# Expert rows of one group by gather from DRAM instead of by matmul, and the last pair's output in three column ranges

## The chip, the cores and the metric

The kernel runs on one core of a Trainium2 chip. The metric is the device time of one execution in microseconds (us), the median of several; lower is better. The engines are TensorE (PE; its weight loads, PEld, run beside the matmuls), VectorE (DVE), ScalarE (ACT), GpSimd (POOL) and SyncE (SP), which here only issues DMAs. Sixteen DMA engines move data between DRAM and the on-chip memory SBUF.

## The reference

One decoder block on 512 tokens of width 1024, float32. Only its last part is touched by the change: a hierarchical mixture of experts over normalised rows, top-1 of 4 groups and then top-2 of 8 SwiGLU experts in it, 32 experts in all, and the final RMSNorm.

```python
x = x + hier_moe(rmsnorm(x, g_moe[l]), ...)
return rmsnorm(x, g_final)

def run_block(args):            # in hier_moe: e expert, tok its tokens, w their weights
    e, tok, w = args
    xb = xt[tok]
    hid = jax.nn.silu(xb @ w_gate[e]) * (xb @ w_up[e])
    return (hid @ w_down[e]) * w[:, None].astype(xb.dtype)
```

Each expert has 1024 x 512 gate and up matrices and a 512 x 1024 down matrix: 6 MB in float32, 201 MB for all 32.

## The kernel before, in words

The order of all instructions on every engine is that of the program text. SBUF blocks of 4 KB a partition (`blk`) come from one pool of 48 (`NB`), middling tiles (`med`) from a pool of 13 (`MB`); an instruction that writes a new tile waits until the earlier user of its buffer is done.

After attention and memory attention the four token tiles `x_sb[t]` (128 tokens x 1024) stay in SBUF, with their scale `r2[t]` (the reciprocal root mean square), and `xrh`, `xrl`, the scaled rows split into a high and a low part. Each expert has 64 slots (`CAP`). `code` holds for each token the code of its two slots, `cw[0]` the same codes broadcast over the partitions, `sid` the code that belongs to each slot.

Experts are worked in 16 pairs (`NP`). Two pairs form a group of 4 experts, 256 slots. For each pair `p`:

- **gate and up**: 8 steps `k`, each with 8 matmul instructions for the pair's two experts (`gate_up`, tile `gu_ps`).
- **hidden**: Silu on ACT, a product on DVE (`hidden`), four transposes (`hidden_t`, tile `ht_ps`). Meanwhile PE does the previous pair's `combine`: products of the slot matrix `ot` with the output rows, split in high and low (`c_ps`), which DVE adds to `x_sb`.
- **down**: 32 instructions (`down`, tile `y_ps`).

The rows of a group (`xT`, features on the partitions) are made by `gather`: for each of 8 feature blocks, 8 matmul instructions of 256 columns take `xrh` and `xrl` times the one-hot matrix `oh` (tile `g_ps`), and ACT scales the result with the gain. Four of the eight blocks are done in the hidden part of the odd pair before the group, four among the first `k` steps of the even pair. Group 0's rows are made before the first pair.

SP issues the expert weights in blocks of 512 KB (tile `we`), 24 for a pair in the order in which they are used: 16 of gate and up, in which each two `k` steps take four blocks, then 8 of down. `eload` lets them run 33 to 35 blocks ahead (`DEPTH`). Experts with more than 64 tokens are finished in a loop (`overflow`, lines 1266 to 1296) that stands at pair 15, `k` = 2 (`SPILL`), and runs zero times in the profiled execution; the third number of `SPILL`, 372, is the count of weight blocks issued before it. The last 12 blocks are issued behind it.

In the last pair the output is made in two halves of 512 columns: down, split, products, addition to `x_sb`, the squares for the final norm, then the scale `r`, and each half of each token tile is written out by a DMA of 256 KB, the low half from ACT's queue, the high half from SP's.

Of the kernel before, what the change touches and what calls it, by code (L numbers as in the profile page):

```python
# [10 lines left out]
F32 = mybir.dt.float32  # L11
# [10 lines left out]
P = 128  # L22
# [21 lines left out]
def _shape_constants():  # L44
    p = np.arange(P)
    tri = ((p[:, None] <= p[None, :]) & (p[:, None] // 64 == p[None, :] // 64)).astype(np.float32)
    upper = (p[:, None] < p[None, :]).astype(np.float32)
    jcode = np.array([ESTR * e + s for e in range(4) for s in range(CAP)], np.int16).view(np.float32)
    e512 = np.arange(NE, dtype=np.float32) * ESTR
    row = np.concatenate([jcode, e512, np.arange(NE, dtype=np.float32), np.arange(NX, dtype=np.float32)])  # L50
    keep = np.concatenate(
        [np.eye(P, dtype=np.float32), np.tile(row, (P, 1)), (ESTR * (p // CAP) + p % CAP).astype(np.float32)[:, None]], axis=1
    )
    onehot = np.zeros((P, 256), np.float32)
    bucket = _t5_buckets()
    for u in range(256):
        onehot[bucket[255 - u], u] += 1.0
        onehot[31, u] -= 1.0
    early = np.concatenate([tri, upper, onehot], axis=1)
    return np.ascontiguousarray(keep), np.ascontiguousarray(early)  # L60


# [8 lines left out]
def block_kernel(ctx, tc, x, mem, g_mem, rel_bias, g_mix, w_in, w_alpha_up, b_alpha, g_gla_head, w_proj_gla,  # L71
# [19 lines left out]
    def blk(name, shape, dt=F32):  # L91
        return bp.tile([P] + list(shape), dt, tag="b", name=name)
# [45 lines left out]
    def tcol(t):  # L138
        return slice(t * P, (t + 1) * P)
# [110 lines left out]
    pslot = keep[:, 320 + NX:321 + NX]  # L250
    first, route = cut(blk("first", [D])), cut(blk("route", [D]))
    early = first([512])
    SY.dma_start(early, c_early)
    tri = early[:, 0:128]
    wup = first([256])[0:17, :]
    SY.dma_start(wup[0:16, :], w_alpha_up)
# [684 lines left out]
    def load_down(e, to=None):  # L941
        for q in range(4):
            b = to[q % len(to)].rearrange("p k n -> p (k n)") if to else blk("we", [D])
            SY.dma_start(b.rearrange("p (k n) -> p k n", k=1), wexp(w_exp_down, e, q, q + 1))
            yield b


    blocks = [[] for _ in range(NE)]
    eloads, elimit = [0], [SPILL[2]]

    def load_pairs():
        for p in range(NE // 2):
            pair = 2 * p, 2 * p + 1
            for loads, n in ((load_gate_up, 2), (load_down, 1)):
                each = [loads(e) for e in pair]
                for q in range(4):
                    for e, load in zip(pair, each):
                        for b in islice(load, n):
                            blocks[e].append(b)
                            yield  # L960
# [184 lines left out]
    S.activation(small("warm", [1]), neghalf[:, 0:1], AF.Silu)  # L1145


    spilled = []

    def spill_list():  # L1150
# [43 lines left out]
    def gather(oh, xT, ns, to=None):  # L1194

        for k in range(KD):
            if len(xT) == k:
                xT.extend(rows2("xT", 4, ns))
            o = to[k % 2] if to else ps("g_ps", [ns])
            for t in range(NT):  # L1200
                for q, src in enumerate((xrh, xrl)):
                    mm(o, src[t][:, tcol(k)], oh[:, t, :], t == 0 and q == 0, t == NT - 1 and q == 1)
            S.activation(xT[k], o, AF.Copy, scale=gfeat[:, k:k + 1])  # L1203
            yield

    def slot_rows(codes, n=P, oa=None):
# [34 lines left out]
    def down(y_ps, hid_t, ft, ws, cs=(0, 1)):  # L1241
        for c in cs:
            for i, (w, own) in enumerate(zip(ws, halves)):
                mm(y_ps[c][own], hid_t[:, ft, 64 * i:64 * i + 64], w[8 + ft][:, 512 * c:512 * c + 512], ft == 0,
                   ft == 3, skip_group_check=True)

    def rows_hilo(y, n=P, parts=None):
        parts = [a[0:n] for a in parts or (med("yh", [512], F32R), med("yl", [512], F32R))]
        split(*parts, y[0:n])
        return parts  # L1250

    def product(o, ot, t, y, first=True):
        for i in range(2):
            mm(o, ot[:, tcol(t)], y[i], first and i == 0, i == 1)
# [42 lines left out]

    NP = NE // 2
    slot, spill = None, spill_list()
    comb, gat = iter(()), iter(())  # L1300
    for p in range(NP):
        w = blocks[2 * p:2 * p + 2]
        used = 24 * p
        depth = DEPTH[min(p, 1)]
        if p == SPILL[0] - 1:
            n_extra = nc.values_load(spilled[0][0:1, 0:1], min_val=0, max_val=NX - 1, skip_runtime_bounds_check_because=
                                     "2 T assignments fill fewer than NX whole blocks")
        eload(used + depth)
        gu = [ps("gu_ps", [512]) for q in range(2)]
        s0 = (p % 2) * P  # L1310
        for k in range(KD):
            if (p, k) == SPILL[0:2]:
                overflow(n_extra, *spilled)
                elimit[0] = 12 * NE
            if p % 2 == 0:
                steps(gat, 1)
            gate_up(gu, k, [xT[k][:, s0 + CAP * i:s0 + CAP * i + CAP] for i in range(2)], w)
            if k % 2:
                eload(used + depth + 2 * (k + 1))
            if p == 0 and k >= BC_AT:  # L1320
                next(bcast, None)
                if k == BC_AT + 1:
                    slot = slot_rows(sid[:, 0:1])
            if p % 2 and p + 1 < NP and k == OH_AT:
                oh_next = group_hots((p + 1) // 2)
        if p % 2 and p + 1 < NP:
            xT = []
            gat = gather(oh_next, xT, 4 * CAP)
        if p == NP - 1:
            gf = blk("gf", [D])  # L1330
            SY.dma_start(gf, bcast_rows(g_final, D))
        hid = hidden(gu, slot[1])
        gs = 1 if p % 2 and p + 1 < NP else 0
        steps(gat, gs)
        steps(comb, 2 if gs else 4)
        hid_t = hidden_t(hid)
        for i in range(3):
            steps(gat, gs)
            steps(comb, 2)
        drain(comb)  # L1340
        ot = slot[0]
        if p + 1 < NP:
            slot = slot_rows(sid[:, 2 * p + 2:2 * p + 3])
        if p >= 2:
            next(spill, None)
        y_ps = [ps("y_ps", [512]) for c in range(2)]
        if p == NP - 1:
            break
        for ft in range(4):
            down(y_ps, hid_t, ft, w)  # L1350
            eload(used + depth + 16 + 2 * (ft + 1))
        ys = {c: rows_hilo(y_ps[c]) for c in range(2)}
        comb = combine(ot, ys)


    ssq, xg, r = [small("ss2", [2]) for t in range(NT)], {}, {}

    def x_half(t, c):
        return x_sb[t][:, 512 * c:512 * c + 512]

    def last_products(c):

        y = rows_hilo(y_ps[c])
        yield
        o = [ps("c_ps", [512]) for t in range(NT)]
        for t in range(NT):
            product(o[t], ot, t, y)
        yield
        for t in range(NT):
            xs = x_half(t, c)  # L1370
            V.tensor_tensor(xs, o[t], xs, op=ALU.add)
            if c == 0 and t == NT - 1:
                yield
            S.activation(blk("sqj", [512]), xs, AF.Square, scale=1.0 / math.sqrt(D), accum_out=ssq[t][:, c:c + 1])
            if c == 0:
                xg[t] = blk("xg", [512])
                G.tensor_tensor(xg[t], xs, gf[:, 0:512], op=ALU.mult)

    def scale(t):
        ms = small("ms", [1])  # L1380
        V.scalar_tensor_tensor(ms, ssq[t][:, 0:1], EPS, ssq[t][:, 1:2], op0=ALU.add, op1=ALU.add)
        r = small("rr", [1])
        G.tensor_tensor(r, ms, neghalf[:, 0:1], op=ALU.pow)
        return r

    def finish(t, r):
        o = blk("xo", [512])
        V.scalar_tensor_tensor(o, x_half(t, 1), r, gf[:, 512:1024], op0=ALU.mult, op1=ALU.mult)
        SY.dma_start(out[tcol(t), 512:1024], o)
        S.activation(xg[t], xg[t], AF.Copy, scale=r)  # L1390
        S.dma_start(out[tcol(t), 0:512], xg[t])

    part = [last_products(c) for c in range(2)]
    for ft in range(4):
        down(y_ps, hid_t, ft, w, (0,))
    next(part[0])
    for ft in range(2):
        down(y_ps, hid_t, ft, w, (1,))
    next(part[0])
    for ft in range(2, 4):  # L1400
        down(y_ps, hid_t, ft, w, (1,))
    next(part[0])
    next(part[1])
    drain(part[0])
    drain(part[1])
    for t in range(NT + 1):
        if t < NT:
            r[t] = scale(t)
        if t:
            finish(t - 1, r[t - 1])  # L1410


WIDE = 2, 2, 2, 2
SPILL = 15, 2, 372
MEM_AT, WOS = (0, 1), {5: 4, 6: 4}
LATE = [], [], range(4)
BC_AT = 2
# [38 lines left out]
```

## Time and profile before

| | |
|---|---|
| time, median of 3 | 970.77 us (969.45 to 970.99) |
| profiled execution, its own time | 969.94 us |
| its span, first to last instruction | 968.1 us |
| granted TensorE clock, mean | 0.997 |
| PE busy | 949.3 us (98%) |
| DVE, ACT, POOL busy | 471.4, 312.2, 32.6 us |
| DMA | 252.47 MB, 261 GB/s over the span |

The expert stage goes from about 486 to 968 us. A busy PE says that some matmul was under way, not that it ran at its peak. The share of DMA in a stretch is the packets' time as a share of 16 engines' time; it can come out a little above 1.

### The profile page before, as it was taken

The page shows a single profiled execution, that of the slowest core. Times are in us where ns is not written, and L with a number is a line of the kernel's source. Part 1 is how long each engine was busy: PE and PEld are TensorE (multiplying, and loading weights), DVE is VectorE, ACT ScalarE, POOL GpSimd, SP SyncE. Part 2 cuts the span into 40 slices and gives each one's busy share as a digit, 9 for nine tenths or more (in the row PEclk, how much of TensorE's full clock was granted, in tenths as well). Part 3 has the DMA queues.
Part 4 walks back from the last instruction along what each step waited for, and adds up shares of the span by engine and source line. Part 5 has one row for each costly group of instructions (what it writes and reads, how often), then busy time and mean ns, then how long its engine had stood idle before and what let it go on. Part 6 is the DMA issues. An engine that isn't in the chain of part 4 may idle for free.

```text
span 968.1 us, 13248 instructions
## 1 busy us (share of the span) xinstructions
PE 949.3 (98%) x4969; PEld 619.2 (64%) x4969; DVE 471.4 (49%) x1047; ACT 312.2 (32%) x639; POOL 32.6 (3%) x46
## 2 busy tenths in 40 slices
PE   9999999999999999999999999999999999999995
PEld 7888888878878888888835445454454543545432
DVE  5344872554557846466733254341544414344234
ACT  6452643545565424455321102111021110201103
POOL 3200010000000000000000000000000000000003
PEclk9999999999999999999999999999999999999998
DMA  9512347223253605482689999999999999999983
GB/s 296 171 44 64 68 68 194 65 66 88 66 196 131 196 1 153 124 336 92 260 339 409 408 409 409 409 409 410 408 410 409 409 408 408 409 408 409 409 317 147
DMA packets 114086, 252.47 MB, mean 261 GB/s; under 512 B 10310, under 2 KB 55651, under 8 KB 114020
## 3 DMA queue, kind: packets, MB, share of 16 engines
q1 hardware_dynamic: 113444, 250.55, 70.2%
q10 hardware_dynamic: 576, 1.05, 0.3%
q8 instruction: 40, 0.66, 0.3%
q14 instruction: 26, 0.21, 0.1%
HBM read 247.90 MB, written 3.67 MB: 260 GB/s over the span
## 4 chain that ended last, share of the span: by engine, by line
PE 92%; DVE 3%; ACT 3%; DMA 1%; issue 1%; ACTq 0%; SPq 0%; DVEq 0%
PE gu_ps L136 22%; PE y_ps L136 12%; PE fo L131 8%; PE fo L133 7%; PE fo L132 7%; PE g_ps L136 7%; PE c_ps L136 6%; PE ro L133 3%; PE ro L131 3%; PE ro L132 3%; PE x2o L136 2%; PE xo L132 1%; PE xo L133 1%; PE xo L131 1%; PE mo_ps L136 1%; PE s_ps L136 1%
## 5 line engine op out<-in xcount | busy, mean ns | idle before, releaser
L136 PE MATMUL gu_ps<-we,xT 128*64 128x512 f32 x1024 | 229.0, 595 | 0.4 <-ACT xT L1045 0.3
L136 PEld LDWEIGHTS gu_ps<-we,xT 128*64 128x64 f32 x1024 | 71.0, 137 | 134.0 <-issue 121.5
L206 DVE TENSOR_TENSOR wlo<-wraw,whi 128x1024 fp32r<-128x1024 f32 (+1 forms) x71 | 86.2, 1231 | 77.2 <-ACT whi L205 76.9
L136 PE MATMUL y_ps<-we,hid_t 128*64 128x512 f32 x512 | 114.2, 596 | 0.7 <-ACT hid_t L1238 0.7
L1230 DVE SCALAR_TENSOR_TENSOR hid<-hid,ws,gu_ps 128x512 f32<-128x512 f32 x16 | 12.0, 747 | 171.2 <-PE gu_ps L136 171.2
L131 PE MATMUL fo<-hTh,whi 128*128 128x512 f32 x224 | 89.1, 398 | 0.0
L132 PE MATMUL fo<-hTl,whi 128*128 128x512 f32 x224 | 87.5, 390 | 0.0
L133 PE MATMUL fo<-hTh,wlo 128*128 128x512 f32 x224 | 87.4, 390 | 0.0
L1263 DVE TENSOR_TENSOR x<-c_ps,x 128x512 f32<-128x512 f32 x120 | 75.0, 683 | 20.7 <-PE c_ps L136 20.7
L136 PEld LDWEIGHTS y_ps<-we,hid_t 128*64 128x64 f32 x512 | 35.9, 137 | 69.8 <-issue 60.0
L205 ACT ACTIVATE whi<-wraw 128x1024 fp32r<-128x1024 f32 (+2 forms) x73 | 74.8, 1045 | 4.2 <-DMA wraw<-in_w_in_dram 4.1
L136 PE MATMUL g_ps<-oh,xrh 128*128 128x256 f32 x256 | 66.0, 299 | 1.4 <-DVE oh L1028 1.4
L136 PEld LDWEIGHTS g_ps<-oh,xrh 128*128 128x128 f32 x256 | 47.0, 189 | 30.7 <-issue 24.3
L136 PE MATMUL g_ps<-oh,xrl 128*128 128x256 f32 x256 | 61.6, 281 | 0.0
L1229 ACT ACTIVATE hid<-gu_ps 128x512 f32<-128x512 f32 x16 | 9.6, 597 | 156.8 <-PE gu_ps L136 156.8
L205 ACT ACTIVATE yh<-y_ps 128x512 fp32r<-128x512 f32 x32 | 19.1, 598 | 115.1 <-PE y_ps L136 115.1
L1203 ACT ACTIVATE xT<-g_ps,gfeat 128x256 f32<-128x256 f32 x56 | 25.8, 474 | 89.2 <-PE g_ps L136 57.6
L136 PE MATMUL c_ps<-yh,ot 128*128 128x512 f32 x128 | 52.0, 406 | 0.7 <-ACT yh L205 0.7
L136 PE MATMUL c_ps<-yl,ot 128*128 128x512 f32 x128 | 50.6, 395 | 0.2 <-DVE yl L206 0.2
L131 PEld LDWEIGHTS fo<-hTh,whi 128*128 128x128 f32 x224 | 42.1, 188 | 10.1 <-issue 1.9
L133 PEld LDWEIGHTS fo<-hTh,wlo 128*128 128x128 f32 x224 | 42.0, 188 | 9.1
L136 PEld LDWEIGHTS g_ps<-oh,xrl 128*128 128x128 f32 x256 | 47.1, 189 | 0.6
(321 smaller groups left out, 1487.4 us busy)
## 6 DMA issues: line engine op xcount, KB each, us to landing
we<-in_w_exp_gate_dram SPq DMA_DIRECT2D x128, 512.0 KB, 10.2
we<-in_w_exp_up_dram SPq DMA_DIRECT2D x128, 512.0 KB, 10.2
we<-in_w_exp_down_dram SPq DMA_DIRECT2D x128, 512.0 KB, 10.2
wraw<-in_w_in_dram SPq DMA_DIRECT2D x38, 512.0 KB, 4.1
wraw<-in_w_out_dram SPq DMA_DIRECT2D x8, 512.0 KB, 5.5
wraw<-in_w_ckv_dram SPq DMA_DIRECT2D x8, 512.0 KB, 4.8
wraw<-in_w_proj_gla_dram SPq DMA_DIRECT2D x4, 512.0 KB, 4.3
wraw<-in_w_proj_moba_dram SPq DMA_DIRECT2D x4, 512.0 KB, 4.4
```

The source lines that it names most:

```text
L131: PE.matmul(o, lh, rh, start=first, stop=False)
L132: PE.matmul(o, lh, rl, start=False, stop=False)
L133: PE.matmul(o, ll, rh, start=False, stop=last)
L136: PE.matmul(o, l, r, start=first, stop=last, **kw)
L205: S.activation(hi, src, AF.Copy)
L206: eng.tensor_tensor(lo, src, f(hi), op=ALU.subtract)
L1203: S.activation(xT[k], o, AF.Copy, scale=gfeat[:, k:k + 1])
L1229: S.activation(row, gu[0][0:n], AF.Silu)
L1230: V.scalar_tensor_tensor(row, row, ws[:, 0:1], gu[1][0:n], op0=ALU.mult, op1=ALU.mult)
L1263: V.tensor_tensor(xs, o, xs, op=ALU.add)
```

## The change

For group 1 (`FETCH`), the scaled rows are written to a DRAM tile `xd` and fetched by token number. ACT makes the rows (`write_rows`) at `k` = 1 to 4 of pair 0, and POOL issues the four writes of 512 KB. A table of token numbers (`tokens`, 256 KB) is loaded by POOL. `fetch` finds on DVE the token of each slot and lets POOL issue one indirect DMA of 128 rows for pair 2 (at pair 0, `k` = 7) and one for pair 3 (at pair 1, `k` = 7), 512 KB each. `turn` transposes the rows on PE in the hidden part of the pair before, two to a step, and ACT scales them with the gain. `gather` and its one-hots are left out for this group. The other groups are as before.

The 372 becomes 376, so four more blocks, the last of gate and up, are issued ahead of the loop. The last pair's down weights come as 8 blocks of two row blocks and 512 columns, first all of the low columns. Its output is worked in column ranges of 512, 256 and 256, the additions and squares are reordered, and three token tiles are written in one DMA of 512 KB each, the fourth in halves.

```diff
+    def load_down_halves(e):
+        for c in range(2):
+            for q in range(2):
+                b = blk("we", [2, 512])
+                rows = w_exp_down[0][e][2 * q * P:(2 * q + 2) * P, 512 * c:512 * c + 512]
+                SY.dma_start(b, rows.rearrange("(k p) n -> p k n", p=P))
+                yield b
...
-            for loads, n in ((load_gate_up, 2), (load_down, 1)):
+            for loads, n in ((load_gate_up, 2), (load_down_halves if p == NE // 2 - 1 else load_down, 1)):
...
+    xd = dp.tile([T, D], F32, name="xd")
+    tok = med("tok", [T])
+    G.dma_start(tok, c_early[:, 512:])
+
+    def write_rows(t):
+        xp = blk("xp", [D])
+        S.activation(xp.rearrange("a (q j p) -> a q j p", p=P, j=2), paired(x_sb[t]), AF.Copy, scale=r2[t])
+        G.dma_start(xd[tcol(t), :], xp)
...
+    def fetch(codes):
+        oa, ws, idx = med("oa", [T]), small("ws", [2]), small("idx", [1], I32)
+        for i in range(2):
+            V.scalar_tensor_tensor(oa, cw[0][:, i, :], codes, tok, op0=ALU.is_equal, op1=ALU.mult,
+                                   accum_out=ws[:, i:i + 1])
+        V.tensor_tensor(idx, ws[:, 0:1], ws[:, 1:2], op=ALU.add)
+        b = blk("rows", [D])
+        G.indirect_dma_start(b, None, xd[:, :], bass.IndirectOffsetOnAxis(ap=idx[:, 0:1], axis=0))
+        return b
+
+    def turn(rows, xT):
+        b = blk("xT", [KD, P])
+        xT.extend(b[:, k, :] for k in range(KD))
+        for k in range(0, KD, 2):
+            t_ps = ps("xt_ps", [2, P])
+            for j in range(2):
+                PE.transpose(t_ps[:, j, :], rows[:, tcol(k + j)], ident)
+            for j in range(2):
+                S.activation(xT[k + j], t_ps[:, j, :], AF.Copy, scale=gfeat[:, k + j:k + j + 1])
+            yield
...
+            if p == 0 and 1 <= k <= NT:
+                write_rows(k - 1)
+            if (p + 2) // 2 in FETCH and k == 7:
+                fetched[p + 2] = fetch(sid[:, 2 * p + 4:2 * p + 5])
-            if p % 2 and p + 1 < NP and k == OH_AT:
+            if p % 2 and p + 1 < NP and k == OH_AT and (p + 1) // 2 not in FETCH:
                 oh_next = group_hots((p + 1) // 2)
-        if p % 2 and p + 1 < NP:
+        if (p + 1) // 2 in FETCH:
+            xT = []
+            gat = turn(fetched.pop(p + 1), xT)
+        elif p % 2 and p + 1 < NP:
...
+    ranges = (0, 512), (512, 256), (768, 256)
...
+    last_down(0, range(4))
+    high(0)
+    low(0)
+    last_down(1, range(4))
+    high(1)
+    low(1)
+    last_down(2, range(2))
+    o0 = products(0)
+    o1 = products(1)
+    last_down(2, range(2, 4))
+    for t in range(NT):
+        add(o0, 0, t)
+        square(0, t)
+        gains(t)
+    for t in range(NT):
+        add(o1, 1, t)
+        if t == 1:
+            high(2)
+        square(1, t)
+        if t == 2:
+            low(2)
+    o2 = products(2)
+    for t in range(NT):
+        add(o2, 2, t)
+        square(2, t)
+        if t >= 2:
+            scale(t - 2)
+    for t in range(NT):
+        if t == 0:
+            scale(2)
+        low_half(t)
+        high_half(t)
+        if t == 0:
+            scale(3)
+        if t + 1 < NT:
+            SY.dma_start(out[tcol(t), :], xo[t])
+    S.dma_start(out[tcol(t), 0:512], xo[t][:, 0:512])
+    SY.dma_start(out[tcol(t), 512:], xo[t][:, 512:])
...
-SPILL = 15, 2, 372
+FETCH = (1,)
+SPILL = 15, 2, 376
```

## Rows read from the trace of the kernel before

**Rows 1.** Table by stretch, the expert stage; last: PE clock, DMA share, GB/s.
```profile
482.00:488.00 6.00, 4.71 (x32) 3.47 (x34) 4.50 (x19) 3.38 (x9) 0.00 (x0) 1.00 0.33 104
488.00:500.00 12.00, 12.00 (x60) 4.23 (x58) 3.21 (x8) 2.04 (x4) 0.00 (x0) 1.00 1.00 382
500.00:915.00 415.00, 413.38 (x2073) 192.67 (x2070) 162.99 (x336) 59.89 (x113) 0.00 (x0) 1.00 1.03 409
```

**Rows 2.** Waits of SP's queue, 565 to 915: us in total, times, longest.
```profile
SPq L938 <- DMA we<-in_w_exp_down_dram: 83.4, 94, 1.6
```

**Rows 3.** Timeline of SP: weight blocks 48, 360, 371, 372, the last eight.
```profile
502.41 0.38 SPq L938 DMA_DIRECT2D we<-in_w_exp_gate_dram  x1
...
903.32 0.33 SPq L938 DMA_DIRECT2D we<-in_w_exp_gate_dram  x1
...
918.12 0.33 SPq L938 DMA_DIRECT2D we<-in_w_exp_up_dram  x1
928.32 0.33 SPq L938 DMA_DIRECT2D we<-in_w_exp_gate_dram  x1
...
930.40 7.32 SPq L944 DMA_DIRECT2D we<-in_w_exp_down_dram  x8
```

**Rows 4.** DMA issues on the page: KB each, us from issue to landing.
```profile
we<-in_w_exp_up_dram SPq DMA_DIRECT2D x128, 512.0 KB, 10.2
```

**Rows 5.** Chain that ended last, pairs 1 to 3: start us, us.
```profile
511.08 13.73 PE gu_ps L136 x64
524.81 1.15 PE g_ps L136 x8
...
526.88 0.44 PE ht_ps L1236 x4
527.32 0.96 PE g_ps L136 x8
...
539.97 1.15 PE g_ps L136 x8
...
570.35 13.73 PE gu_ps L136 x64
```

**Rows 6.** The same chain, pair 15.
```profile
925.32 3.46 PE gu_ps L136 x16
...
929.93 7.41 DMA we<-in_w_exp_up_dram
...
937.38 2.79 PE gu_ps L136 x10
940.17 2.05 PE c_ps L136 x8
...
944.50 5.87 PE y_ps L136 x24
```

**Rows 7.** Waits of SP's queue, 915 to 940, at the loop.
```profile
SPq L1267 <- PEq L1267: 7.5, 2, 7.3
```

**Rows 8.** Timeline of ACT at the start of pair 0.
```profile
485.77 1.57 ACT L1045 ACTIVATE xT<-g_ps,gfeat 128x256 f32<-128x256 f32 x4
```

**Rows 9.** Instructions of line 925: ns least, median, most.
```profile
L925 ACT ACTIVATE xrh<-x,rr x4: 1217/1220/1222, 443.9 to 476.2; 128x1024 fp32r<-128x1024 f32 x4
```

**Rows 10.** Timeline of POOL from 480; in brackets its idle time before.
```profile
951.90 5.01 POOL L1377 TENSOR_TENSOR xg<-x,gf 128x512 f32<-128x512 f32 x4 [475.74 <-DVE x L1371]
```

**Rows 11.** Timeline of the last part.
```profile
953.05 0.61 ACT L1374 ACTIVATE sqj<-x 128x512 f32<-128x512 f32 x1
...
960.23 3.11 SPq L1389 DMA_DIRECT2D out_dram<-xo  x4
...
963.69 0.34 ACTq L1391 DMA_DIRECT2D out_dram<-xg  x1
```

**Rows 12.** Table by stretch, the output written from two queues.
```profile
962.00:963.00 1.00, 0.00 (x0) 0.00 (x0) 0.79 (x2) 0.58 (x2) 0.00 (x0) 0.81 1.04 385
966.00:967.00 1.00, 0.00 (x0) 0.00 (x0) 0.00 (x0) 0.00 (x0) 0.00 (x0) 0.50 0.62 225
```

More of the change, by code (lines that the diff above doesn't have):

```diff
@@ L58, in _shape_constants @@
         onehot[31, u] -= 1.0
-    early = np.concatenate([tri, upper, onehot], axis=1)
+    tokens = np.tile(np.arange(T, dtype=np.float32), (P, 1))
+    early = np.concatenate([tri, upper, onehot, tokens], axis=1)
     return np.ascontiguousarray(keep), np.ascontiguousarray(early)
@@ L252, in block_kernel @@
     early = first([512])
-    SY.dma_start(early, c_early)
+    SY.dma_start(early, c_early[:, 0:512])
     tri = early[:, 0:128]
@@ L1299, in block_kernel @@
     slot, spill = None, spill_list()
-    comb, gat = iter(()), iter(())
+    comb, gat, fetched = iter(()), iter(()), {}
     for p in range(NP):
@@ L1309, in block_kernel @@
         gu = [ps("gu_ps", [512]) for q in range(2)]
-        s0 = (p % 2) * P
+        s0 = 0 if p // 2 in FETCH else (p % 2) * P
         for k in range(KD):
@@ L1332, in block_kernel @@
         hid = hidden(gu, slot[1])
-        gs = 1 if p % 2 and p + 1 < NP else 0
+        gs = 1 if (p % 2 or p // 2 in FETCH) and p + 1 < NP else 0
         steps(gat, gs)
@@ L1353, in block_kernel @@
         comb = combine(ot, ys)
[L1356 to L1365, printed above, removed]
-        for t in range(NT):
[L1367 to L1377, printed above, removed]
+    ranges = (0, 512), (512, 256), (768, 256)
@@ new lines, in block_kernel, with x_part, y_part, last_down @@
+    ssq, xo = [small("ss4", [4]) for t in range(NT)], [blk("xo", [D]) for t in range(NT)]
+    r = [small("rr", [1]) for t in range(NT)]
+    for t in range(NT):
+        V.memset(ssq[t][:, 3:4], EPS)
+    y_ps.append(ps("y_ps", [256]))
+    def x_part(i, t):
+        a, n = ranges[i]
+        return x_sb[t][:, a:a + n]
+    def y_part(i):
+        return y_ps[i][:, 0:ranges[i][1]]
+    def last_down(i, fts):
+        a, n = ranges[i]
+        c, a = divmod(a, 512)
+        for ft in fts:
+            for e, (b, own) in enumerate(zip(w, halves)):
+                mm(y_ps[i][own, 0:n], hid_t[:, ft, 64 * e:64 * e + 64], b[8 + 2 * c + ft // 2][:, ft % 2, a:a + n],
+                   ft == 0, ft == 3, skip_group_check=True)
@@ new lines, in block_kernel, with high, low, products @@
+    y = [[med(q, [n], F32R) for q in ("yh", "yl")] for _, n in ranges]
+    def high(i):
+        S.activation(y[i][0], y_part(i), AF.Copy)
+    def low(i):
+        V.tensor_tensor(y[i][1], y_part(i), f(y[i][0]), op=ALU.subtract)
+    def products(i):
+        n = ranges[i][1]
+        o = [ps("c_ps", [512 // n, n]) for _ in range(NT * n // 512)]
+        o = [b[:, q, :] for b in o for q in range(512 // n)]
+        for t in range(NT):
+            product(o[t], ot, t, y[i])
+        return o
@@ L1379, in scale, with add, square, gains @@
+    def add(o, i, t):
+        V.tensor_tensor(x_part(i, t), o[t], x_part(i, t), op=ALU.add)
+    def square(i, t):
+        S.activation(blk("sqj", [512])[:, 0:ranges[i][1]], x_part(i, t), AF.Square, scale=1.0 / math.sqrt(D),
+                     accum_out=ssq[t][:, i:i + 1])
+    def gains(t):
+        G.tensor_tensor(xo[t][:, 0:512], x_part(0, t), gf[:, 0:512], op=ALU.mult)
     def scale(t):
         ms = small("ms", [1])
-        V.scalar_tensor_tensor(ms, ssq[t][:, 0:1], EPS, ssq[t][:, 1:2], op0=ALU.add, op1=ALU.add)
@@ L1382, in scale @@
[L1382 to L1410, printed above, removed]
+        V.tensor_reduce(ms, ssq[t], axis=AX.X, op=ALU.add)
+        G.tensor_tensor(r[t], ms, neghalf[:, 0:1], op=ALU.pow)
@@ new lines, in low_half, with high_half @@
+    def low_half(t):
+        S.activation(xo[t][:, 0:512], xo[t][:, 0:512], AF.Copy, scale=r[t])
+    def high_half(t):
+        V.scalar_tensor_tensor(xo[t][:, 512:], x_sb[t][:, 512:], r[t], gf[:, 512:], op0=ALU.mult, op1=ALU.mult)
+    last_down(0, range(4))
[12 more added lines that the diff above has]
+        gains(t)
@@ new lines, in block_kernel @@
+    for t in range(NT):
[11 more added lines that the diff above has]
+            scale(t - 2)
+    for t in range(NT):
+        if t == 0:
[6 more added lines that the diff above has]
+            SY.dma_start(out[tcol(t), :], xo[t])
```

## Prediction

> **What bounds the kernel now.** I read the page first, then the table by stretch, the chain that ended last, the waits of SP's queue and its timeline. The page alone misleads: PE is busy for 98% of the span, so it looks like the one bound, and taking matmuls from it looks like a gain of their full length. The table by stretch says that the DMA engines are full as well: from 500 to 915 us their share is 1.03 at 409 GB/s, while from 488 to 500 they moved 382 GB/s and from 482 to 488 only 104 [rows 1]. At 409 GB/s a weight block of 524,288 bytes takes 1.28 us. SP's waits say the same from the other side: between 565 and 915 its queue stood for earlier weight blocks, 83.4 us of it for one kind of them alone, hardly for PE [rows 2].
>
> So two streams run side by side, and what counts is which is ahead. PE takes a pair of experts in half of 570.35 − 511.08, that is 29.6 us [rows 5]; DMA needs 24 blocks × 1.28 = 30.8. PE is the faster one and lives on blocks that were loaded ahead. Block 48, the first of pair 2, is issued at 502.41 [rows 3] and lands 10.2 later [rows 4], at 512.6; PE uses it from 541.1, behind the gather piece at 539.97 [rows 5]: 28.5 us in hand. Block 360, the first of pair 15, is issued at 903.32 [rows 3], lands at 913.5 and is used at 925.32 [rows 6]: 11.8 us in hand. 13 pairs ate 16.7 us of the lead.
>
> In pair 15 the lead ends. Block 371 is issued at 918.12 and 372 only at 928.32 [rows 3], since the last 12 stand behind the loop, where SP waits 7.3 us for PE [rows 7]. Block 375, the last of gate and up, lands at 929.93 + 7.41 = 937.3, and PE's last 10 gate-and-up instructions hang on it: they start at 937.38, and the pair's first combine product follows at 940.17, the down part at 944.50 [rows 6]. From there to the end of the span (968.1) it is 23.6 us.
>
> **The gather of group 1.** Removed: eight pieces of 8 matmuls, four in the hidden part of pair 1 (1.15, then three at 0.96) and four at 1.15 in pair 2 [rows 5], together 8.6 us. Added: 16 transposes, at 0.44 for four [rows 5] 1.8 us, and some 0.6 for eight changes between kinds of matmul: 2.4 (bounds 1.8 and 3.0). PE is then 6.2 us earlier from pair 3 on (5.6 to 6.8). That is a gain only as far as weights are there.
>
> **The DMAs that come with it.** Four writes of 512 KB, two gathers of 512 KB: 3.15 MB. The 256 KB of token numbers come before pair 0, where the engines are little used (482 to 488, [rows 1]); nothing waits for them before the first fetch, so I cost them at nothing, and at 0.6 us without that cover. The writes can't come there: ACT makes the rows in program order behind the xT scaling that begins at 485.77 [rows 8], the first about 489, and each takes about the 1.22 of the like instruction [rows 9]. They meet full engines. No row shows POOL issuing a DMA. The nearest is the output, where two queues write together: share 1.04, 385 GB/s [rows 12], not more than the 409 of one. So I take the queues as sharing one capacity: 3.15 MB / 409 = 7.7 us, less 0.4 for the room between 382 and 409 in 488 to 500 (12 us × 27 GB/s is 0.3 MB, 0.8 us; I take half), so 7.3 us by which every later weight block is late. Bounds: 0, if a second queue could add its bytes to the first one's; 10, if the writes run at 385 (8.2) and four buffers lent to the rows leave the engines without a load for 2 us. I take the sharing, because the row with two queues is the nearest there is.
>
> Here a rule speaks against the change. The Trainium skill, DMA: Bandwidth & Descriptors, section "Issuing engines are not separate DMA queues", says that transfers started by SP, ACT or POOL run on the same 16 engines and interleave, so another issuer saves issue time alone. The output row agrees (385 with two queues). By that rule the added bytes cost 7.7 us of the stream; with queues of their own capacity they would cost nothing.
>
> **Block 375.** With 376 ahead of the loop the gap of 10 us is gone: block 372 follows 371 after 1.28, so 375 would land at 918.12 + 4 × 1.28 + 10.2 = 933.4 without the added bytes and at 940.7 with them; before it was 937.3. PE, 6.2 us early, wants it at about 931 and waits some 10 us, spread over the last pairs: its lead on this block was 3.5 (it wants it in the second half of `k` = 6, after 6.75 steps of 13.73 / 8 = 1.72 [rows 5], at 936.9, against 933.4), less 6.2, less 7.3. So PE's gain is wholly lost, and the end of gate and up moves by 940.7 − 937.3 = +3.4 us.
>
> The moved loop also turns its wait round. SP now reaches it only after issuing 375 (923.3 + 7.3 = 930.6), and if the engines meet there, PE stands until about 931 to 933 before `k` = 2. From 933 it has four steps of 1.72 to `k` = 6, 939.9, just ahead of block 375: no cost, but 1 us more in SP would be one.
>
> The eight half down blocks follow at 1.28, the last at about 951.4 (951.9 if rows of 2 KB go at 385). Down starts at 944.50 + 3.4 = 947.9, its first half lasts 3.5, and the last blocks are wanted at 952.3. No cost.
>
> **The small edits.** DVE's token search for pair 2 stands before pair 0's hidden part, where DVE waits for PE (it works 3.21 of the 12 us from 488 to 500 [rows 1]); that for pair 3 likewise, and the group's one-hots fall away. POOL is idle from 476 to 952 [rows 10], so its six issues hide whatever they cost up to several us each; the rows for pair 2 are wanted at 525, a good 20 us after the fetch. ACT's four row makings take 4.9 us of the 12 from 488 to 500, of which it worked 2.04 [rows 1]. Behind them in ACT's order stand the copies of the weights' broadcast and pair 0's Silu, and DVE's slot weights wait for those. If a row tile had no buffer, these would be late by one release, some 2 us, and PE with them; at the end PE waits 10 us for DMA, which covers it.
>
> **The last part.** PE's columns are the same, in more instructions. ACT's squares go from 8 at 0.61 [rows 11] to 4 at 0.61 and 8 of half width at about 0.4 (an estimate from the same row), 5.6 instead of 4.9, with the third range's high copy among them. I place the squares' end 14.6 us after down starts, the first output issue at 15.5 (before 960.23, 15.7), the last at 17.8 (before 963.69, 19.2 [rows 11]), since one DMA of 512 KB now follows another after 0.75 instead of 1.15. But 2.1 MB take 5.5 us at 385 [rows 12], so the bytes end it: 15.5 + 0.8 + 5.5 + 1.5 (before, the bytes ended about 966.6 [rows 12], the span at 968.1) = 23.3, against 23.6. I take −0.4. Bounds: −1.5 if the last issue ends it, +1.0 if matmuls of half width stand for their weight loads.
>
> **Sum.** +3.4 − 0.4 = +3.0 us on the profiled execution's 969.94, so 972.9. The median shown, 970.77, is 0.8 above that execution; on it the change gives 973.8, which I predict.
>
> **Rivals.** (A) The other sign: the POOL transfers don't hold up the weights. Then 375 lands at 933.4, the end of gate and up moves by −3.9, with the tail −4.3: 966.5. It decides from the point where the added bytes cost under 3.9 us of the stream; under 2.4 it is faster by over 0.2%. For it: no row shows POOL's transfers, and the weight blocks alone, without the gap at the loop, would come 3.9 us earlier [rows 3]. Against it: 1.03 and 409 hold for 415 us [rows 1], and two queues gave no more [rows 12]. Chance 0.26. (B) It nets out: bytes at 6.9, gate and up +3.0, the tail at its better bound −1.5, and a landing estimate 1 us too late: about +0.5, 971.3. Chance 0.22. (C) A new wait on top: lent buffers leave DMA idle for 2 us or more, or the engines stand at the loop until SP has issued 375 and PE loses 2 us there: bytes at 10 or the like, +6 and more, 976.5. For it: until 500 SP's loads wait for PE's buffers, which is why 482 to 488 was empty [rows 1]; against it: at the writes DMA has their own bytes to move. Chance 0.08.
>
> **How the numbers follow.** The forecast (DMA bound in pairs 13 to 15, +2 to +5 us) has 0.44. Its own range is 972.7 to 976. A measurement of this kernel tells 0.2%, 1.9 us, from no change. Faster: A, 0.26. Within: B, and a little of the forecast's lower edge, 0.24. Slower: the rest, 0.50. The range of 966 to 977 leaves out the lower part of A and the upper of C, under 2 in 10.
>
> **What would show it.** Right: in the profile after, 409 GB/s from 500 on without a break; PE with several us of idle time in pairs 12 to 15, released by weight DMAs; no gap in SP's issues at 918 to 928; block 375 issued near 930 and landing near 941; gate and up of pair 15 ending near 944. PE's pairs 2 and 3 together some 6 us shorter. Wrong, if PE has no DMA waits in the last pairs, if the weight blocks after 500 are issued less than 4 us later than before, or if over 430 GB/s are moved where POOL's writes run. If gate and up end as forecast and the total differs, it is the last part that I have mis-sized.

## The result and the profile after

The change makes the kernel slower. Its median is 976.29 us (975.05 to 977.04, 5 runs) against 970.77 (969.45 to 971.51, 5 runs): a ratio of 1.0058 with a 95% interval of 1.0047 to 1.0070. Forecast were 973.8 us, a range of 966 to 977, and 0.50 for slower. So the direction held and the time lies in the range, but the size is off: +5.5 us instead of +3.0. The likeliest case's own range, which ended at 976, missed it by 0.3.

The profiled execution took 975.67 us, its span is 973.9 (before 968.1), so +5.8 are to be found. The table by stretch comes first, as in [rows 1]:

```profile
482.00:488.00 6.00, 4.66 (x32) 3.47 (x34) 4.50 (x19) 3.33 (x9) 0.00 (x0) 1.00 0.46 164
488.00:500.00 12.00, 12.00 (x60) 4.20 (x58) 4.86 (x14) 4.26 (x6) 1.11 (x2) 1.00 0.94 347
500.00:520.00 20.00, 16.50 (x68) 5.36 (x66) 6.55 (x15) 4.60 (x6) 2.09 (x3) 0.83 1.01 396
520.00:930.00 410.00, 407.01 (x2016) 189.75 (x2014) 163.02 (x332) 60.09 (x120) 0.97 (x1) 1.00 1.03 409
930.00:940.00 10.00, 7.42 (x38) 2.61 (x36) 0.69 (x1) 0.00 (x0) 0.00 (x0) 1.00 1.02 403
```

The same view of the kernel before, where [rows 1] doesn't split the stretch:

```profile
500.00:520.00 20.00, 18.38 (x88) 6.15 (x86) 7.30 (x18) 2.39 (x4) 0.00 (x0) 1.00 1.02 409
```

The DMA engines stay full at 409 GB/s, as before, until 930 and beyond. New are three things: less was moved from 488 to 500 (347 GB/s; 382 before), PE is idle for 3.5 us from 500 to 520 (1.6 before) at a granted clock of 0.83, and it is idle for 2.6 us from 930 to 940. SP's timeline says what the stream lost; block 96 is the first of pair 4, behind all writes and gathers:

```profile
573.45 0.33 SPq L939 DMA_DIRECT2D we<-in_w_exp_gate_dram  x1
...
913.00 0.33 SPq L939 DMA_DIRECT2D we<-in_w_exp_gate_dram  x1
...
927.05 0.33 SPq L939 DMA_DIRECT2D we<-in_w_exp_up_dram  x1
...
932.16 0.33 SPq L939 DMA_DIRECT2D we<-in_w_exp_up_dram  x1
935.22 8.48 SPq L954 DMA_DIRECT2D we<-in_w_exp_down_dram  x8
```

Block 96 is issued at 573.45; the same view of the kernel before has it at 563.59. Block 360 stands 9.7 later than in [rows 3], block 371 8.9 later. Block 375 follows at 932.16, and the last eight at 935.22. So the loss is made before 574 and carried to the end.

Where it is made, the timelines of ACT and of POOL show (the bracket gives the idle time before the instruction and what ended it):

```profile
493.39 1.22 ACT L1164 ACTIVATE xp<-x,rr 128x1024 f32<-128x1024 f32 x1 [4.48 <-PE gu_ps L137]
...
500.94 2.32 ACT L1164 ACTIVATE xp<-x,rr 128x1024 f32<-128x1024 f32 x2 [4.19 <-PE gu_ps L137]
503.16 0.59 ACT L1272 ACTIVATE hid<-gu_ps 128x512 f32<-128x512 f32 x1
```

```profile
494.92 0.57 POOL L1165 DMA_DIRECT2D xd<-xp  x1 [17.88 <-ACT xp L1164]
...
502.46 0.53 POOL L1165 DMA_DIRECT2D xd<-xp  x1 [5.37 <-ACT xp L1164]
...
514.39 1.02 POOL L1234 DMA_INDIRECT rows<-xd,idx  x1 [10.30 <-DMA we<-in_w_exp_down_dram]
```

ACT had no buffer for the rows until PE had finished with weights: it waited twice for `gu_ps`, 4.48 and 4.19 us. The rows took four of the 48 buffers that the weight stream lives on, and the writes went out at 495 to 504, into full engines. SP in turn had to wait for these writes to land before it could load weights into the four buffers again; its waits from 484 to 520 (us in total, times, longest):

```profile
SPq L945 <- DMA xd<-xp: 6.5, 2, 5.0
SPq L939 <- DMA xd<-xp: 2.9, 1, 2.9
```

Pair 0's Silu, behind the rows on ACT, starts at 503.16. PE pays at once:

```profile
504.58 1.11 PE L1279 MATMUL ht_ps<-keep,hid 128*128 128x128 f32 x4 [2.81 <-DVE hid L1273]
506.38 9.44 PE L137 MATMUL y_ps<-we,hid_t 128*64 128x512 f32 x32 [0.69 <-ACT hid_t L1281]
515.66 2.74 PE L137 MATMUL gu_ps<-we,xT 128*64 128x512 f32 x12
...
818.32 1.08 PE L137 MATMUL gu_ps<-we,xT 128*64 128x512 f32 x4 [1.03 <-DMA we<-in_w_exp_gate_dram]
```

It stood 2.81 and 0.69 us (0.93 and 0.69 before), and from 504 to 512 the granted clock was 0.54 to 0.60 in the table by stretch, partly the lower of its two levels (1.2 and 2.4 GHz), so the down part took 9.44 us (7.09 before). Pair 1 starts at 515.66, in the same view of the kernel before at 510.91, so 4.75 later. That looks dear, but the weights end later still, and it is gone by pair 11, where PE waits for weight blocks (the last row, one of them).

The end of the kernel, first the instructions of the loop's line (sequencers, with first and last start), then the chain that ended last, then SP's first output issues:

```profile
L1310 SPq EVENT_SEMAPHORE  x28: 17/17/17, 932.5 to 935.1; - x28
L1310 PEldq EVENT_SEMAPHORE  x8: 51/51/51, 928.2 to 935.1; - x8
...
L1310 PEldq COMPARE_BRANCH  x2: 97/204/310, 933.8 to 933.9; - x2
```

```profile
935.21 10.90 PE gu_ps L137 x48
946.11 2.05 PE c_ps L137 x8
...
950.44 6.17 PE y_ps L137 x40
```

```profile
965.46 1.72 SPq L1500 DMA_DIRECT2D out_dram<-xo  x3
```

PE's part of the loop begins at 928.2, SP comes at 932.5, behind block 375, and all leave at 935.1: PE, which before had made SP wait there for 7.3 us [rows 7], now waits for SP, 2.58 us without work. Gate and up end at 946.11, in [rows 6] at 940.17, so +5.9. The chain shows no wait in these 48 instructions, but the weight loads do, a short one, and the DMA issues from 930 to 945 give the time to landing of block 375:

```profile
943.32 0.21 PEld L137 LDWEIGHTS gu_ps<-we,xT 128*64 128x64 f32 x3 [0.22 <-DMA we<-in_w_exp_up_dram]
```

```profile
we<-in_w_exp_up_dram SPq DMA_DIRECT2D x1, 512.0 KB, 11.1
```

Block 375, issued at 932.16, lands 11.1 us later, at 943.3, and releases the last ten instructions, which need 2.79: 946.1. So it is block 375 that sets the end here, and not the stand at the loop: from 935.21 PE alone needs 48/64 of run 1's 13.90 us and would have been done at 945.6. From the down part to the end it is 973.9 − 950.44 = 23.5, before 23.6. The sum is +5.8.

### The profile page after: what moved, and what is told of

It reads as the page before. It is cut to its first block, busy times and chain, and to the rows that moved or that the text cites. A ratio compares the mean times of both kernels' runs of the same rounds, so it can differ in the third digit from the quotient of the medians.

```text
span 973.9 us, 13250 instructions
## 1 busy us (share of the span) xinstructions
PE 947.4 (97%) x4945; PEld 618.1 (63%) x4945; DVE 472.0 (48%) x1057; ACT 318.1 (33%) x660; POOL 37.9 (4%) x53
## 5 line engine op out<-in xcount | busy, mean ns | idle before, releaser
L137 PEld LDWEIGHTS gu_ps<-we,xT 128*64 128x64 f32 x1024 | 73.9, 137 | 140.9 <-issue 117.8
L137 PE MATMUL y_ps<-we,hid_t 128*64 128x512 f32 (+1 forms) x528 | 116.0, 592 | 1.3 <-ACT hid_t L1281 1.0
L137 PE MATMUL g_ps<-oh,xrh 128*128 128x256 f32 x224 | 57.5, 299 | 1.4 <-DVE oh L1038 1.4
L137 PEld LDWEIGHTS g_ps<-oh,xrh 128*128 128x128 f32 x224 | 40.9, 189 | 26.5 <-issue 21.1
L137 PE MATMUL g_ps<-oh,xrl 128*128 128x256 f32 x224 | 53.7, 281 | 0.0
L137 PE MATMUL c_ps<-yh,ot 128*128 128x512 f32 (+1 forms) x132 | 52.9, 402 | 0.7 <-ACT yh L1431 0.7
L137 PE MATMUL c_ps<-yl,ot 128*128 128x512 f32 (+1 forms) x132 | 51.0, 388 | 0.1
L132 PEld LDWEIGHTS fo<-hTh,whi 128*128 128x128 f32 x224 | 42.1, 188 | 10.1 <-issue 1.9
L133 PEld LDWEIGHTS fo<-hTl,whi 128*128 128x128 f32 x224 | 42.1, 188 | 8.0
L1223 ACT ACTIVATE xT<-g_ps,gfeat 128x256 f32<-128x256 f32 x48 | 22.1, 474 | 76.5 <-PE g_ps L137 49.4
## 6 DMA issues: line engine op xcount, KB each, us to landing
we<-in_w_exp_gate_dram SPq DMA_DIRECT2D x128, 512.0 KB, 10.2
we<-in_w_exp_up_dram SPq DMA_DIRECT2D x128, 512.0 KB, 10.2
we<-in_w_exp_down_dram SPq DMA_DIRECT2D x128, 512.0 KB, 10.2
```

The source lines that it names most:

```text
L132: PE.matmul(o, lh, rh, start=first, stop=False)
L133: PE.matmul(o, lh, rl, start=False, stop=False)
L137: PE.matmul(o, l, r, start=first, stop=last, **kw)
```

## The experiments

All are timed in rounds beside the kernel before, whose median there was 970.83 to 970.89 us.

**1. Without the fetch.** All of the change but group 1's rows: 376, the half down blocks and the column ranges stay.

```diff
-FETCH = (1,)
+FETCH = ()
... (also taken out: xd, tok, write_rows and its calls)
```

> The change without the fetch: no row writes, no token table, group 1 gathered by matmul as before; 376 blocks ahead of the loop, half down blocks and the column ranges stay. Theory 1 (the weight stream sets the end; the fetch's bytes and lent buffers made it about 9.9 us late): the stream is on the time of before, block 375 is issued near 923, PE is the bound to the end of gate and up near 939.5, total 969.0 to 970.5, ratio 0.998 to 1.000. Rival (the last part in column ranges, or the meeting at the loop with 376, costs by itself): 973 or more, ratio 1.003 or more.

Measured: 968.17 us, ratio 0.9971 (0.9960 to 0.9982). This version beats both kernels. SP's and PE's timelines:

```profile
923.78 0.33 SPq L939 DMA_DIRECT2D we<-in_w_exp_up_dram  x1
928.39 6.67 SPq L954 DMA_DIRECT2D we<-in_w_exp_down_dram  x8
```

```profile
925.21 13.90 PE L137 MATMUL gu_ps<-we,xT 128*64 128x512 f32 x64
```

Block 375 goes out at 923.78, SP is at the loop before PE, and PE works through all 64 instructions without a wait. Gate and up end at 939.11, 1.1 earlier than in [rows 6], and the last part takes 22.8 instead of 23.6. So all of the loss is the fetch's.

**2. The fetch alone.** The kernel before with group 1's fetch; 372, whole down blocks and the old last part. Read against the change:

```diff
-SPILL = 15, 2, 376
+SPILL = 15, 2, 372
... (the last part and load_down as in the kernel before)
```

> The fetch alone on the kernel before: 372 ahead of the loop, whole down blocks, the old last part. Theory 1: block 96 is issued 9 to 10 us later than before; with 372 the loop is met after block 371 near 927, the last 12 blocks follow from about 933, gate and up end near 945, total 975 to 977, ratio 1.005 to 1.007, as the whole change. Rival (the last part or the loop makes the loss): within 1 us of before, ratio 0.999 to 1.001.

Measured: 975.61 us, ratio 1.0049 (1.0036 to 1.0063). SP's timeline, then PE's:

```profile
573.57 0.33 SPq L939 DMA_DIRECT2D we<-in_w_exp_gate_dram  x1
...
926.30 0.33 SPq L939 DMA_DIRECT2D we<-in_w_exp_up_dram  x1
```

```profile
942.48 2.79 PE L137 MATMUL gu_ps<-we,xT 128*64 128x512 f32 x10 [0.20 <-DMA we<-in_w_exp_up_dram]
```

The stream is as late as in the whole change (block 96 at 573.57, block 371 at 926.30), and pair 15's last ten instructions are released by a weight block. The two parts don't add up: alone they give +4.8 and −2.7, together +5.5. What 376 and the last part bring without the fetch isn't there when the stream is 8 us late.

**3. Rows from the split high part.** POOL writes `xrh`, which exists by 477, so ACT makes nothing and no buffer is lent for it. The fetched rows lack the low part, here, in run 4 and in the second kernels of runs 7 and 8.

```diff
-        xp = blk("xp", [D])
-        S.activation(xp..., paired(x_sb[t]), AF.Copy, scale=r2[t])
-        G.dma_start(xd[tcol(t), :], xp)
+        G.dma_start(xd[tcol(t), :], f(xrh[t]))
```

> The change with the rows written straight from xrh, the rounded high part that lies in SBUF anyway (the fetched rows lack the low part): the same bytes at the same place in the program, but no ACT work and no lent buffers. Theory 1, bytes: block 96 is issued 7.0 to 7.9 us later than before instead of 9.9, the engines meet at the loop about 2 us sooner, total about 974.2, ratio 1.0035 (1.0025 to 1.0045). Rival 2 (the loss is PE's: pair 0's Silu 2.2 us late behind the row making, PE idle and its clock halved for some 7 us): that is gone, PE keeps its gain of 6 us, total 966 to 970, ratio under 0.9995.

Measured: 971.33 us, ratio 1.0004 (0.9995 to 1.0013), no change against the kernel before, and 2.9 under the expectation. The profiled execution took 972.41, 1.1 above the median. POOL's timeline, the table by stretch, SP's timeline, PE's:

```profile
477.15 2.14 POOL L1163 DMA_DIRECT2D xd<-xrh  x4
```

```profile
482.00:488.00 6.00, 4.55 (x32) 3.47 (x34) 4.51 (x18) 3.21 (x9) 0.00 (x0) 1.00 1.03 412
```

```profile
566.82 0.33 SPq L939 DMA_DIRECT2D we<-in_w_exp_gate_dram  x1
```

```profile
929.52 13.29 PE L137 MATMUL gu_ps<-we,xT 128*64 128x512 f32 x48 [3.38 <-PEq L1308]
```

I had not seen that the writes would now go out at 477, into the stretch in which the engines had moved 104 GB/s [rows 1]; they moved 412 there. Against run 1 (564.18), block 96 is 2.6 later: 1.05 MB of gathers at 409 GB/s are 2.6. The four writes cost the stream nothing where the engines were empty. But this run changes two things at once, so the next one separates them.

**4. The same writes, held.** POOL waits for a broadcast at 494 before it issues them: the time of the change's writes, still no ACT work and no lent buffer.

```diff
+        if t == 0:
+            G.tensor_copy(small("hold", [1]), cw[1][:, 0, 0:1])
         G.dma_start(xd[tcol(t), :], f(xrh[t]))
... (the four calls also stand one step later, at k = 2 to 5)
```

> The rows written from xrh, but POOL is held until ACT's copy of the weights' broadcast in pair 0 (about 494), so that the same 2.1 MB go out when the change writes them; no lent buffers, no ACT work. The place of block 96 tells bytes from buffers: 570.8 to 571.5 (7.2 to 7.9 late) if the bytes cost their time in the full stretch and the lent buffers made the other 2 us; 573.4 if the buffers cost nothing; 567 if bytes in the full stretch are nearly free. PE stands at the loop (step 2) for 3 us or more and loses clock, total 974 to 979.

Measured: 976.74 us, ratio 1.0059 (1.0043 to 1.0074). POOL's timeline, SP's, and the table by stretch:

```profile
494.92 2.16 POOL L1165 DMA_DIRECT2D xd<-xrh  x4
```

```profile
572.18 0.33 SPq L939 DMA_DIRECT2D we<-in_w_exp_gate_dram  x1
```

```profile
488.00:500.00 12.00, 12.00 (x60) 4.08 (x56) 5.02 (x14) 2.26 (x4) 2.79 (x5) 1.00 0.97 344
500.00:520.00 20.00, 18.37 (x88) 6.22 (x86) 6.54 (x15) 2.39 (x4) 1.03 (x1) 1.00 1.03 417
934.00:936.00 2.00, 1.80 (x6) 0.71 (x8) 0.00 (x0) 0.00 (x0) 0.00 (x0) 0.57 1.04 414
```

Moved by 18 us, the same bytes cost 5.4 us more stream (572.18 − 566.82) and 5.4 us of time. PE does not stand in pair 0 here, and the time is that of the change: pair 0's stall is covered, as forecast. Block 96 is 1.3 earlier than in the change, and 0.7 later than forecast for lent buffers that cost 2 us. This run drops the lent buffers, ACT's rows and the stand in pair 0 together. What points to the buffers is SP's queue: the change waits there for the rows' writes, 6.5 and 2.9 us, this run for none, and from 500 to 520 the change moved 396 GB/s, this run 417. From 488 to 500 the two don't differ (347 and 344).

**5. Each write twice.** The second goes to a tile that nobody reads.

```diff
         G.dma_start(xd[tcol(t), :], xp)
+        G.dma_start(xd2[tcol(t), :], xp)
```

> The whole change, with each of the four row writes issued twice, the second time to a DRAM tile that nobody reads. 2.1 MB more in the full stretch, and nothing else for the engines but that each lent buffer is held until its second write has landed. Theory 1 (the 16 engines have one capacity, and each added byte delays the weight stream by its share of 409 GB/s): 5.1 us more stream, 375 issued near 937.3 instead of 932.2; gate and up end at least 5.1 later, near 951.3, more if the engines' meeting at the loop grows as with two groups; time 981.5 to 985. Rival (it is the buffers, the indirect transfers or ACT that delay the stream, and the writes as such ride along): 375 within 1.5 us of 932.2, time 976 to 978.

Measured: 981.07 us, ratio 1.0102 (1.0085 to 1.0119), 0.4 under the expectation's range. SP's timeline:

```profile
578.22 0.33 SPq L939 DMA_DIRECT2D we<-in_w_exp_gate_dram  x1
...
936.47 0.33 SPq L939 DMA_DIRECT2D we<-in_w_exp_up_dram  x1
```

2.1 MB more make block 96 4.8 later, block 375 4.3 and the time 4.8; 2.1 MB / 409 are 5.1. The rival, that writes ride along, falls.

**6. Two groups.** Group 2 is fetched as well, from the same rows: two more gathers, 1 MB.

```diff
-FETCH = (1,)
+FETCH = (1, 2)
```

> The change with groups 1 and 2 fetched: two more gathers (1.05 MB), another 64 gather matmuls out of PE, no further writes. Theory 1: the stream is 2.6 us later still, PE only waits longer, total 978 to 979.5, ratio 1.0075 to 1.009. Rival 2 (PE's time is the bound): PE 6 us earlier still, total 970 to 972, ratio near 1.000.

Measured: 985.95 us, ratio 1.0150 (1.0135 to 1.0166), 6.4 us above all that I had expected. Block 375 is 2.9 later than with one group, as the bytes say. The rest is at the loop, by PE's timeline and the loop's line:

```profile
943.55 1.97 PE L137 MATMUL gu_ps<-we,xT 128*64 128x512 f32 x4 [8.33 <-PEq L1310]
```

```profile
L1310 PEldq COMPARE_BRANCH  x2: 101/3096/6090, 936.6 to 936.8; - x2
```

PE stood 8.33 us, behind one branch of its sequencer that took 6.09; in the change the longer of the two takes 0.31. After it the granted clock was 0.50, and 48 instructions took 13.0 us instead of 10.4. Why the branch took so long isn't settled: one more packet of the instruction queue falls in this stretch than in the change, and the weight queue was full, but I made no run for it.

**7. The loop at step 6.** Once for the whole change, once for run 3's kernel.

```diff
-SPILL = 15, 2, 376
+SPILL = 15, 6, 376
```

> The whole change with one number different: the loop stands at step 6 of pair 15 instead of step 2. Theory 3 (at the loop the engines wait for SP, which comes only after issuing block 375, and 2.6 us more for the meeting itself; PE stood 2.6 us there): PE no longer stands at the loop, gate and up end when block 375 (landing near 942.4) lets them, near 945.2 instead of 946.1, total 975.3, 0.9 less than the whole change. Rival (the meeting costs nothing, the stream alone sets the end): 976.3. Rival 2 (the last eight blocks, now issued about 940, come too late): 977 or more.

> The rows written from xrh (no lent buffers, no ACT work, written from 477 on), with the loop at step 6. With the loop at step 2 PE stood 3.4 us there and then worked at half its clock for a while; 375 was issued at 926.5. Theory 3: both go away, gate and up end about 939.5 instead of 942.8, total 968.0 to 969.5, ratio 0.997 to 0.999. Rival (stream alone): no change against 971.3.

Measured: 975.89 us (ratio 1.0048, 1.0034 to 1.0061) and 971.05 (1.0005, 0.9995 to 1.0014), only 0.4 and 0.3 under the kernels with the loop at step 2, a difference that the intervals don't tell from none. SP's and PE's timelines of the whole change with the loop at 6:

```profile
939.73 5.74 SPq L954 DMA_DIRECT2D we<-in_w_exp_down_dram  x8
```

```profile
942.41 2.79 PE L137 MATMUL gu_ps<-we,xT 128*64 128x512 f32 x10 [0.20 <-DMA we<-in_w_exp_up_dram]
...
955.31 1.94 PE L137 MATMUL y_ps<-we,hid_t 128*64 128x256 f32 x14 [0.60 <-DMA we<-in_w_exp_down_dram]
```

PE no longer stands at the loop, and gate and up end at 945.2 (942.41 + 2.79), when block 375 allows it. That is 0.9 before the change, where it was block 375 as well: issued at 932.29, it lands after 10.1 us here and after 11.1 there. Why, no run shows. But the last eight blocks, behind the loop, go out at 939.73, 4.5 later than in the change, PE waits for one of them at 955.31, and the first 40 instructions of down take 7.8 us instead of 6.2. What gate and up gave back, down took.

**8. Rows written early and exactly.** Unscaled rows and their scales (a [128, 1] tile) are written between 443 and 477, both are fetched, ACT scales after the fetch; loop at step 6.

```diff
+        G.dma_start(xd[tcol(t), :], x_sb[t])
+        G.dma_start(rd[tcol(t), :], r2[t])
...
+        rs = small("rs", [1])
+        for to, src in ((b, xd), (rs, rd)):
+            G.indirect_dma_start(to, None, src[:, :], ...)
```

> The exact rows, written before the scaling: POOL writes each tile of x and its scale to DRAM as soon as they are there (443 to 480, where DMA has room), the fetch takes the scale along, ACT scales the fetched rows in place; loop at step 6. By the stream theory only the two gathers (1.05 MB, 2.6 us) are left in the full stretch: block 96 near 566.2, 375 issued near 926, gate and up end near 939, total 968 to 969.5, ratio 0.997 to 0.999, about that of the change without the fetch (0.9971). If the gain of PE counted instead: 963 to 965.

Measured: 980.34 us, ratio 1.0095 (1.0079 to 1.0110): the expectation falls. The DMA engines were full without moving much, by the table by stretch:

```profile
448.00:452.00 4.00, 4.00 (x26) 3.53 (x25) 3.48 (x20) 0.00 (x0) 0.00 (x0) 1.00 0.95 86
```

I suspected the scales, 128 pieces of 4 bytes, and measured them by themselves: run 3 with the four writes of scales alone.

```diff
+        G.dma_start(rd[tcol(t), :], r2[t])
```

> The rows written from the already split high part (the fetched rows lack the low part), as in the run that wrote them straight away (971.33 us; weight block 96 issued at 566.82), and besides POOL writes the four scales, 128 rows of 4 bytes each, to DRAM between 443 and 477. Nothing reads them there. Theory (the 4-byte rows are what held the DMA engines with little throughput in the run with unscaled rows): between 443 and 500 shares near 0.9 at about 100 GB/s again, block 96 near 575, time 977 to 980. Rival (they cost nothing beside 512 KB transfers; it was the unscaled rows' own writes ahead of the gating that collided): block 96 within 1 us of 566.8, time 970.5 to 972.

Measured: 980.65 us, ratio 1.0113 (1.0091 to 1.0136), 9.3 us above run 3, for 2 KB in all. The table by stretch of this run and then of run 3, the row of DMA issues and SP's timeline:

```profile
472.00:480.00 8.00, 7.75 (x65) 7.28 (x64) 6.04 (x26) 3.76 (x7) 3.80 (x7) 1.00 0.85 139
```

```profile
472.00:480.00 8.00, 7.75 (x64) 7.26 (x63) 6.06 (x26) 3.76 (x7) 3.51 (x6) 1.00 0.99 388
```

```profile
rd<-rr POOLq DMA_DIRECT2D x4, 0.5 KB, 8.6
```

```profile
574.50 0.33 SPq L939 DMA_DIRECT2D we<-in_w_exp_gate_dram  x1
```

139 GB/s in place of 388, with the engines 0.85 busy; a write of 0.5 KB takes 8.6 us to land, and block 96 comes 7.7 later, near the forecast 575. So the theory holds against its rival, though the time is 0.65 above its range. The Trainium skill, DMA: Bandwidth & Descriptors, "Specifications", gives 512 bytes as the least transfer at full rate and says that a smaller one is a read-modify-write. The low rate agrees; a read-modify-write no row here shows.

## Why the prediction came out as it did

**The weights set the end, PE's gain is lost.** Right. The stretch from 520 to 930 runs at 409 GB/s; without the fetch (run 1) PE has more matmuls to do and the kernel is still 8.1 faster. PE's gain itself came as forecast: from the start of pair 1 to that of pair 4 it needs 82.85 us (515.66 to 598.51) instead of 89.41 (510.91 to 600.32), 6.6 less (forecast 6.2, 5.6 to 6.8). Of the 10 us of waiting that were forecast for it, 4.75 went into pair 0; then it was idle for 3.0 before 930, 2.3 of it for weight blocks, and for 2.6 at the loop.

**One capacity for all queues.** Right, and the step that carries the forecast. Runs 3 and 4 differ in when the same 2.1 MB are written: 5.4 us. Run 5 doubles them: 4.8. For the whole fetch I had 7.3 us by which later blocks are late. Run 4, with its bytes in the full stretch and no lent buffer, has block 375 at 931.15, run 1 at 923.78: 7.4. That they agree so closely is partly luck: by block 96 it is 8.0 (572.18 against 564.18), and the room from 488 to 500, for which I had taken off 0.4, wasn't filled (344 GB/s in run 4, 382 before).

**Lent buffers.** Mis-sized. I put them at nothing and kept 2 us for the outer bound. ACT waited 4.48 and 4.19 us for buffers, SP 9.4 for the writes out of them, and block 375 is issued 1.0 later than in run 4 (block 96, 1.3). That this is the buffers and not ACT's work rests on SP's waits and on 500 to 520 (396 against 417 GB/s); no run takes away the buffers alone.

**Block 375.** Mis-sized, by 2.5 us. Forecast were an issue at 930.6 and a landing at 940.7. It was issued at 932.16, 1.6 later: 0.1 by the bytes, 1.0 by the lent buffers, and 0.5 in the stream without any fetch (923.78 in run 1, where the prediction had derived 923.3). That 0.5 arises from 488 to 500, where run 1 moved 365 GB/s and the kernel before 382; why, no run explains. And it landed 11.1 us after its issue, at 943.3, where I had taken the median of 10.2 [rows 4]: 0.9 more. In run 3 and in both kernels of run 7 it took 10.1, in run 5 11.0; what decides that is open.

**"No cost" at the loop.** Right for the change, but not by the margin that I gave. The prediction had the engines meet, PE stand until 931 to 933, and PE back just ahead of block 375, with 1 us more in SP as a cost. PE stood until 935.2: SP came 1.6 later than forecast, and the meeting took 2.6 us after it arrived, for which the sum had no term. It stayed without cost because block 375 came 2.5 later itself. The kernel before has such a meeting too, 2.0 us from the last engine's arrival (DVE, 926.2) to 928.2, but PE worked through it. What the stand cost follows from the landing of block 375 plus the 2.79 of the ten instructions behind it, against the measured end of gate and up:

| kernel | 375 issued | lands | end by the weights | end measured | difference |
|---|---|---|---|---|---|
| change | 932.16 | 943.3 | 946.1 | 946.11 | 0.0 |
| run 3 | 926.47 | 936.6 | 939.4 | 942.81 | +3.4 |
| run 4 | 931.15 | 941.3 to 942.3 | 944.0 to 945.0 | 946.42 | +1.4 to 2.4 |
| run 5 | 936.47 | 947.5 | 950.3 | 951.73 | +1.5 |
| run 6 | 935.04 | 945.1 to 946.1 | 947.9 to 948.9 | 956.57 | +7.6 to 8.6 |
| run 7, whole change | 932.29 | 942.4 | 945.2 | 945.2 | 0.0 |
| run 7, rows from `xrh` | 926.44 | 936.5 | 939.3 | 939.35 | 0.0 |
| run 8, scales alone | 934.16 | 945.2 | 947.9 | 949.42 | +1.5 |

For runs 4 and 6 the profile gives no landing; the bounds are the 10.1 and 11.1 us of the other rows. With the loop at step 2, 1.4 to 8.6 us are lost in these profiles in every other kernel that has the fetch and 376, and these are the ones in which PE's granted clock fell after the stand, to 0.50 to 0.58 in stretches of 2 us; in the change it stayed at 1.00. At step 6 nothing is lost there, but then the down blocks are late. In run 1 SP is there before PE, and nothing is lost.

**The last part.** Forecast −0.4 (its own terms give −0.3), measured −0.1 in the change and −0.8 in run 1. The first output was issued 15.0 us after down starts (forecast 15.5). What took it back in the change is the end, 8.4 us from there instead of 7.9 in run 1. All nine kernels that have the fetch and the new last part show 8.4 to 8.5, so it comes with the fetch; why is open. In the change one packet of an instruction queue is moved between the landing of the output and the end of the span, in run 1 none, but no run tests that.

**The sum.** +3.4 − 0.4 was forecast. Measured are 3.4 + 1.6 (block 375's issue) + 0.9 (its landing) = +5.9, and −0.1 for the last part: +5.8 in the span, +5.5 in the medians.

**The rivals.** A, that POOL's transfers don't hold up the weights, falls by runs 2, 4 and 5. B falls with it. C had 0.08: lent buffers that leave the engines without a load, or a stand at the loop on top, and 976.5. Both happened beside the forecast's own mechanism: the lent buffers at about 1 us, the stand at 2.6, which in the change was hidden behind block 375 and cost nothing. I had set a chance for the two as a mishap, where I should have added the first as a term and given the second a price: ACT's need for a buffer and the order "375, then the loop" stand in the program. That the time comes out at C's 976.5 all the same is chance: the rest is block 375's slower landing and the stream's 0.5.

**Pair 0's stall.** I had about 2 us, covered. PE stood 1.9 us longer than before (3.5 against 1.6), and through the clock it was 4.75 at the start of pair 1. It was covered all the same: by pair 11 PE waits for weights, and run 4, which has no such stall, ends no earlier (though it also lost 1.4 us or more at the loop).

## What to carry to other kernels

Where the DMA engines are full to the end, as here, count work that is moved from PE into DMA at its bytes divided by the full rate, also when another engine's queue issues it (runs 4 and 5: 4.3 to 5.4 us for 2.1 MB, 5.1 by the rate). Such bytes were free only in a stretch with room, so when a write goes out can count for as much as its size (run 3 against run 4: 5.4 us for 18 us of delay). Before a transfer is given a buffer from the pool that the load stream runs on, the stream's loss belongs in the sum. And when more loads are issued ahead of a point where all engines meet, ask which engine will now be the last to come, and what is issued behind it. A stand that the profile shows need not be a loss: look for what releases the work behind it, down to waits of 0.2 us.

## What the runs showed of the hardware that I had not expected

- Four writes of 128 pieces of 4 bytes from POOL's queue, 2 KB in all, beside 512 KB transfers: 9.3 us of time, with DMA shares of 0.85 at 139 GB/s.
- A loop that runs zero times still took 2.6 to 3.4 us of PE's time when SP came last, and 8.3 once, with one branch of 6.09 us. In the change the stand was hidden behind block 375's landing.
- A stand at the loop did not always cost the same clock. In the change PE stood 2.58 us and the granted clock stayed at 1.00; in run 5 it stood 2.58 as well and the clock was 0.50 from 942 to 944; in run 4 it was 0.57 from 934 to 936 after 3.0. What tells them apart, no run shows. The row is run 5's:

```profile
942.00:944.00 2.00, 2.00 (x6) 0.60 (x4) 0.00 (x0) 0.00 (x0) 0.00 (x0) 0.50 1.01 372
```
